# Moving one large store from the Pool queue to the SP queue in a mixture-of-experts kernel

## The chip, the cores and the metric

The kernel runs on one core of one Trainium2 chip. The metric is the device time of one execution in microseconds (us); the kernel before takes 181.32 us, the median of three runs that lie between 181.3 and 181.46. The profile is one further execution taken with the hardware profiler. Its span runs from the first to the last instruction of the core, 179.7 us, a little less than the device time (181.48 us for that execution).

The engines are TensorE (PE, matrix products, with PEld for the loading of its stationary operand), VectorE (DVE), ScalarE (ACT), GpSimd (POOL) and SyncE (SP). Transfers between the chip's main memory and the on-chip memory are issued here by Pool, whose transfers run in a software-made queue (q0 in the profile), or by SP, whose transfers run in a hardware-made queue (q1).

## The reference

Eight experts, each a pair of matrix products with a ReLU between them. Inputs and outputs are fp32.

```python
n_experts, capacity, hidden, expert_hidden = 8, 256, 512, 2048
x:  (8, 256, 512)
w1: (8, 512, 2048)
w2: (8, 2048, 512)

def reference(x, w1, w2):
    h = np.matmul(x, w1)
    h = np.maximum(h, 0)
    return np.matmul(h, w2).astype(np.float32)
```

The weights are 2 x 8 x 512 x 2048 x 4 bytes = 67 MB, which have to be read once; x and the output are 4.2 MB each.

## The kernel before

Pool issues all weight loads. They cast fp32 to bf16 on the way. The experts are loaded in pairs, with the last pair split into single experts and the last w2 into two halves; `tail` is the second half of w2 of expert 7, held back from the list.

```python
GROUPS = [(0, 1), (2, 3), (4, 5), (6, 7)]
W1_LOADS = [(g,) for g in GROUPS[:-1]] + [((6,),), ((7,),)]
W2_LOADS = [(g, 0, K2) for g in GROUPS[:-1]] + [((6,), 0, K2), ((7,), 0, 8), ((7,), 8, K2)]
# ... (cut)
x_v   = x.rearrange("e (pp r) k -> (e pp) (r k)", r=R)
w2_v  = w2.rearrange("e (p j) n -> p e (j n)", p=P)
out_v = out.rearrange("e (p mo) k -> p e (mo k)", mo=MC)
# ... (cut)
out_sb   = const.tile([P, E - 1, MC, H], FP32, name="out_sb")    # experts 0 to 6
out_last = const.tile([P, MC, H], FP32, name="out_last")         # expert 7

def load_w2(es, a, b):
    # ... (cut: picks the group's tile)
    nc.gpsimd.dma_start(
        w2t[g][:, i:i + len(es), a * H:b * H],
        w2_v[:, es[0]:es[-1] + 1, a * H:b * H],
    )

def store_first():
    nc.gpsimd.dma_start(
        out_v[:16, 0:5:2, :16], out_sb[:16, 0:5:2, 0, :16]
    )

def store():
    nc.gpsimd.dma_start(
        out_v[:, :E - 1, :], out_sb[:].rearrange("p e m h -> p e (m h)")
    )
```

`store_first` is the small store: 16 partitions, three experts, 16 numbers each, 3 KB. It writes to a part of the output that `store` writes again, so `store` has to wait until the small store has landed. `store` is the big store: the outputs of experts 0 to 6, 3584 KB, one contiguous row of 4 KB for each partition and expert.

The second layer accumulates over k = 0 to 15 in two row blocks m. For the last expert k is the outer loop, so the tail (k = 8 to 15) is needed from the middle on:

```python
if last:
    order = [(k, m) for k in range(K2) for m in range(MC)]
else:
    order = [(k, m) for m in range(MC) for k in range(K2)]
for k, m in order:
    nc.tensor.matmul(o_ps[m][:], hT[:, k, m * P:(m + 1) * P],
                     w2t[g][:, e - g[0], k * H:(k + 1) * H],
                     start=(k == 0), stop=(k == K2 - 1))
    if k == K2 - 1:
        if last and m == 1:
            nc.scalar.copy(out_last[:, m, :], o_ps[m][:])
        elif last:
            nc.vector.tensor_copy(out_last[:, m, :], o_ps[m][:])
        else:
            nc.vector.tensor_copy(out_sb[:, e, m, :], o_ps[m][:])
```

The main loop, in which the orders of Pool and of TensorE are as written:

```python
nc.sync.dma_start(x_head[:], x_v[:, :HEAD * H])
# ... (cut)
for i, g in enumerate(GROUPS):
    # ... (cut: loads issued as buffers come free; first layer of pairs)
    for e, hT in zip(g, hs):
        layer2(e, hT or layer1(e))
        if e == 5:
            issue(E, E)            # all remaining loads but the tail
            store_first()
            loads.append(tail)
            issue(E, E)            # the tail
        if e == E - 2:
            store()
nc.sync.dma_start(out_v[:, E - 1, :], out_last[:].rearrange("p m h -> p (m h)"))
```

So Pool's queue ends with: loads, small store, tail, big store. SP issues two transfers: a part of x at the start and the last expert's output at the end.

Of the kernel before, what the change touches and what calls it, by code (L numbers as in the profile page):

```python
# [14 lines left out]
def kernel(  # L15
# [7 lines left out]
    nc = tc.nc  # L23
# [69 lines left out]
        )  # L93

    def store():
        nc.gpsimd.dma_start(  # L96
            out_v[:, :E - 1, :], out_sb[:].rearrange("p e m h -> p e (m h)")
        )

# [38 lines left out]
    def layer2(e, hT):  # L138
# [7 lines left out]
        for k, m in order:  # L146
# [7 lines left out]
            if k == K2 - 1:  # L154
# [3 lines left out]
                    nc.vector.tensor_copy(out_last[:, m, :], o_ps[m][:])  # L158
                else:
                    nc.vector.tensor_copy(out_sb[:, e, m, :], o_ps[m][:])  # L160

    loads = []
# [19 lines left out]
    with tc.manual_schedule(engines={mybir.EngineType.PE, mybir.EngineType.Pool}):  # L184
        load_x()
        make_identity(nc, identity)
        issue(B, B - 1)
        transpose_x()
        for i, g in enumerate(GROUPS):
            issue(i + B, i + B)  # L190
            whole = len(g) > 1 and (g,) in W1_LOADS
            if whole:
                hs = [layer1(e) for e in g]
                issue(i + 1 + B, i + B)
            else:
                hs = [None] * len(g)
# [3 lines that stand above are left out]
                    issue(E, E)  # L200
                    store_first()
                    loads.append(tail)
                    issue(E, E)
                if e == E - 2:
                    store()
# [30 lines left out]
```

## Time and profile before

| What | Value |
|---|---|
| device time, median of 3 | 181.32 us |
| span of the profiled execution | 179.7 us |
| TensorE busy | 127.1 us (71%) |
| ScalarE busy | 44.1 us (25%) |
| VectorE busy | 16.5 us (9%) |
| read from main memory | 71.30 MB |
| written to main memory | 4.20 MB |
| share of q0 (Pool) in the 16 transfer engines' span | 96.8% |
| share of q1 (SP) | 2.4% |

The page cuts the span into 40 slices of 4.49 us. A digit is the busy share of a slice in tenths; the rate in GB/s counts bytes as written. A line of the chain of waits gives shares of the span by what the chain passed through. A line of the list of issues gives the tile and tensor, the issuing queue, the count, the size of each and the us from issue to landing. A line of the timeline gives start, duration, engine, source line and operation, and in brackets the idle time before it with what ended it. A line of the transfer records gives the queue, its packets, MB and its share of the 16 engines in the window asked for.

In the kernel before, L91 is the small store, L83 the loads of w2, L96 the big store, L147 the matmuls of the second layer, L160 the copies of experts 0 to 6 into out_sb, L206 the store of the last output.

### The profile page before, as it was taken

The page shows a single profiled execution, that of the slowest core. Times are in us where ns is not written, and L with a number is a line of the kernel's source. Part 1 is how long each engine was busy: PE and PEld are TensorE (multiplying, and loading weights), DVE is VectorE, ACT ScalarE, POOL GpSimd, SP SyncE. Part 2 cuts the span into 40 slices and gives each one's busy share as a digit, 9 for nine tenths or more (in the row PEclk, how much of TensorE's full clock was granted, in tenths as well). Part 3 has the DMA queues.
Part 4 walks back from the last instruction along what each step waited for, and adds up shares of the span by engine and source line. Part 5 has one row for each costly group of instructions (what it writes and reads, how often), then busy time and mean ns, then how long its engine had stood idle before and what let it go on. Part 6 is the DMA issues. An engine that isn't in the chain of part 4 may idle for free.

```text
span 179.7 us, 1827 instructions
## 1 busy us (share of the span) xinstructions
PE 127.1 (71%) x824; PEld 90.5 (50%) x832; DVE 16.5 (9%) x20; ACT 44.1 (25%) x70; POOL 9.9 (6%) x20
## 2 busy tenths in 40 slices
PE   0017600899629991999569943999199999999960
PEld 0017500699514440899434412999034479469520
DVE  0205500000001111000002210000002210110010
ACT  2004400266500000266500000566100026116210
POOL 7000100000100001000100030000002000002000
PEclk9999975699978999699999997899969999999998
DMA  6999998999999899999999999999999999999995
GB/s 201 252 219 204 233 230 186 226 233 208 201 233 230 190 222 233 208 201 233 230 193 219 233 208 201 233 230 193 219 233 204 204 233 228 195 210 214 349 420 217
DMA packets 3735, 40.48 MB, mean 225 GB/s; under 512 B 272, under 2 KB 272, under 8 KB 1296
## 3 DMA queue, kind: packets, MB, share of 16 engines
q0 software_dynamic: 3440, 38.80, 96.8%
q1 hardware_dynamic: 288, 1.57, 2.4%
q8 instruction: 6, 0.10, 0.2%
q14 instruction: 1, 0.01, 0.0%
HBM read 71.30 MB, written 4.20 MB: 420 GB/s over the span
## 4 chain that ended last, share of the span: by engine, by line
PE 58%; DMA 27%; another core or an unknown queue 9%; POOL 1%; issue 1%; ACT 0%; POOLq 0%
PE o_ps L147 32%; DMA w_sb<-in_w_dram 27%; PE h_ps L124 25%; POOL w_sb L76 0%; POOL w_sb L69 0%; ACT out_last L156 0%; POOL identity masks.py:199 0%; POOL identity masks.py:197 0%; POOLq masks.py:199 0%; POOLq L220 0%
## 5 line engine op out<-in xcount | busy, mean ns | idle before, releaser
L124 PE MATMUL h_ps<-xT,w_sb 128*128 128x256 bf16 x512 | 61.3, 285 | 20.2 <-DMA w_sb<-in_w_dram 20.2
L124 PEld LDWEIGHTS <-w_sb 128*128 128x128 bf16 x512 | 58.3, 146 | 24.1 <-DMA w_sb<-in_w_dram 21.9
L147 PE MATMUL o_ps<-w_sb,hT 128*128 128x512 bf16 x248 | 58.6, 393 | 12.8 <-DMA w_sb<-in_w_dram 12.2
L131 ACT ACTIVATE hT<-h_ps 128x512 bf16<-128x512 f32 x64 | 38.2, 597 | 106.8 <-PE h_ps L124 106.8
L147 PEld LDWEIGHTS <-hT 128*128 128x128 bf16 x256 | 25.6, 101 | 44.3 <-issue 9.3
L160 DVE COPY out_sb<-o_ps 128x512 f32<-128x512 f32 x14 | 9.7, 692 | 128.7 <-PE o_ps L147 128.7
L107 PE MATMUL xt_ps<-identity,w_sb 128*128 128x128 bf16 x64 | 7.7, 309 | 13.8 <-DVE w_sb L183 6.9
L107 PEld LDWEIGHTS <-w_sb 128*128 128x128 bf16 x64 | 6.7, 145 | 14.6 <-DVE w_sb L183 6.9
L111 ACT COPY xT<-xt_ps 128x1024 bf16<-128x1024 bf16 x4 | 4.0, 1012 | 16.5 <-PE xt_ps L107 16.5
L83 POOL DMA_DIRECT2D w_sb<-in_w_dram x6 | 3.8, 637 | 53.6 <-PE o_ps L147 36.5
L113 DVE COPY xT<-xt_ps 128x1024 bf16<-128x1024 bf16 x4 | 4.9, 1224 | 10.2 <-PE xt_ps L107 10.2
L76 POOL DMA_DIRECT2D w_sb<-in_w_dram x5 | 3.3, 658 | 44.6 <-PE h_ps L124 44.6
L96 POOL DMA_DIRECT2D out_dram<-out_sb x1 | 1.0, 968 | 27.3 <-issue 27.3
L91 POOL DMA_DIRECT2D out_dram<-out_sb x1 | 0.6, 554 | 29.2 <-DVE out_sb L160 29.2
L156 ACT COPY out_last<-o_ps 128x512 f32<-128x512 f32 x1 | 0.6, 585 | 6.3 <-PE o_ps L147 6.3
L158 DVE COPY out_last<-o_ps 128x512 f32<-128x512 f32 x1 | 0.7, 692 | 13.4 <-PE o_ps L147 13.4
L183 DVE CAST w_sb<-x_head 128x2048 bf16<-128x2048 f32 x1 | 1.2, 1228 | 5.6 <-DMA x_head<-in_x_dram 5.6
L111 ACT ACT_TABLE_LOAD x1 | 1.3, 1283 | 0.7 <-PEq L220 0.7
L69 POOL DMA_DIRECT2D w_sb<-in_x_dram x1 | 0.7, 679 | 0.8 <-POOLq L220 0.8
masks.py:199 POOL TENSOR_SCALAR_AFFINE_SELECT identity<-identity 128x128 bf16<-128x128 bf16 x1 | 0.3, 287 | 0.1
masks.py:197 POOL MEMSET identity<- 128x128 bf16 x1 | 0.2, 223 | 0.0
L220 POOL MEMSET const-float32-0.0<- 128x1 f32 x1 | 0.1, 93 | 0.2 <-issue 0.2
(3 smaller groups left out, 0.3 us busy)
## 6 DMA issues: line engine op xcount, KB each, us to landing
w_sb<-in_w_dram POOLq DMA_DIRECT2D x6, 4096.0 KB, 62.1
w_sb<-in_w_dram POOLq DMA_DIRECT2D x3, 2048.0 KB, 51.5
out_dram<-out_sb POOLq DMA_DIRECT2D x1, 3584.0 KB, 12.9
w_sb<-in_w_dram POOLq DMA_DIRECT2D x2, 1024.0 KB, 44.7
w_sb<-in_x_dram POOLq DMA_DIRECT2D x1, 1536.0 KB, 11.6
x_head<-in_x_dram SPq DMA_DIRECT2D x1, 1024.0 KB, 4.8
out_dram<-out_last SPq DMA_DIRECT2D x1, 512.0 KB, 4.3
out_dram<-out_sb POOLq DMA_DIRECT2D x1, 3.0 KB, 27.8
```

What stands on the lines that cost most here:

```text
L69: nc.gpsimd.dma_start(x_sb[:, HEAD * H:], x_v[:, HEAD * H:])
L76: nc.gpsimd.dma_start(w1t[g][:, i:i + len(es), :], w1_v[:, es[0]:es[-1] + 1, :])
L83: nc.gpsimd.dma_start(w2t[g][:, i:i + len(es), a * H:b * H], w2_v[:, es[0]:es[-1] + 1, a * H:b * H],)
L96: nc.gpsimd.dma_start(out_v[:, :E - 1, :], out_sb[:].rearrange("p e m h -> p e (m h)"))
L107: nc.tensor.transpose(ps[:, r2, :], x_r[:, r2, m, :, ko], identity[:])
L111: nc.scalar.copy(dst, src)
L113: nc.vector.tensor_copy(dst, src)
L124: nc.tensor.matmul(h_ps[:, s, :], w1_r[:, ko, :, j], xT[:, ko, :, e, :], start=(ko == 0), stop=(ko == K1 - 1),)
L131: nc.scalar.activation(hT[:, pr * 2:pr * 2 + 2, :].rearrange("p a c -> p (a c)"), h_ps[:].rearrange("p a c -> p (a c)"), mybir.ActivationF ...
L147: nc.tensor.matmul(o_ps[m][:], hT[:, k, m * P:(m + 1) * P], w2t[g][:, e - g[0], k * H:(k + 1) * H], start=(k == 0), stop=(k == K2 - 1),)
L160: nc.vector.tensor_copy(out_sb[:, e, m, :], o_ps[m][:])
L183: nc.vector.tensor_copy(x_sb[:, :HEAD * H], x_head[:])
```

## The change

The big store is issued by SP instead of Pool. Its place among the calls, its source and its target stay. It still has to wait until the small store has landed, as both write the same rows, and until VectorE has copied expert 6. What it is for: Pool's queue holds the tail between the small store and the big store; from SP's queue the big store can start when the small store has landed, beside the tail. On SP it stands ahead of the store of the last output.

```diff
     def store():
-        nc.gpsimd.dma_start(
+
+
+        nc.sync.dma_start(
             out_v[:, :E - 1, :], out_sb[:].rearrange("p e m h -> p e (m h)")
         )
```

Everything else is the same but for blank lines, which move the line numbers. TensorE, VectorE and ScalarE get the same instructions in the same order; Pool has one transfer less and SP one more.

## The prediction

> **What bounds the kernel now.** I read the slices of the page first, then the chain of waits, the list of transfers by issue, the timeline of the last 45 us, and last the transfer records in short windows around the two points where the queues meet.
>
> ```profile
> PE   0017600899629991999569943999199999999960
> DMA  6999998999999899999999999999999999999995
> GB/s 201 252 219 204 233 230 186 226 233 208 201 233 230 190 222 233 208 201 233 230 193 219 233 208 201 233 230 193 219 233 204 204 233 228 195 210 214 349 420 217
> PE 58%; DMA 27%; another core or an unknown queue 9%; POOL 1%; issue 1%; ACT 0%; POOLq 0%
> ```
>
> The reader is to see that the transfer engines are at 9 tenths in practically every slice and that TensorE has holes. The chain names TensorE for 58%, but that is work hung between arrivals of weights; the transfers never rest. The rate counts bytes as written, and the weights are cast from fp32 to bf16 on the way, so 233 GB/s of weights is 466 GB/s read. In slices 38 and 39 the rate is 349 and 420: there the seven stored outputs pass, fp32 to fp32. A kernel whose transfers are full from the second slice to the last ends when the sum of the bytes has passed, in whatever order, unless the order leaves a hole.
>
> ```profile
> out_dram<-out_sb POOLq DMA_DIRECT2D x1, 3584.0 KB, 12.9
> w_sb<-in_w_dram POOLq DMA_DIRECT2D x1, 1024.0 KB, 32.0
> out_dram<-out_last SPq DMA_DIRECT2D x1, 512.0 KB, 4.3
> out_dram<-out_sb POOLq DMA_DIRECT2D x1, 3.0 KB, 27.8
> ```
>
> These are the issues after 130 us, the last number being us from issue to landing. With the starts on the timeline they give four landings:
>
> ```profile
> 136.36 0.55 POOL L91 DMA_DIRECT2D out_dram<-out_sb  x1 [29.16 <-DVE out_sb L160]
> 136.91 0.57 POOL L83 DMA_DIRECT2D w_sb<-in_w_dram  x1
> 164.73 0.97 POOL L96 DMA_DIRECT2D out_dram<-out_sb  x1 [27.26 <-issue]
> 166.80 7.07 PE L147 MATMUL o_ps<-w_sb,hT 128*128 128x512 bf16 x31
> 174.51 0.35 SPq L206 DMA_DIRECT2D out_dram<-out_last  x1
> ```
>
> The small store lands at 136.36 + 27.8 = 164.2, the tail (second half of w2 of expert 7) at 136.91 + 32.0 = 168.9, the big store at 164.73 + 12.9 = 177.6, the last expert's output at 174.51 + 4.3 = 178.8. The span ends at 179.7. So the big store waits for the small one already: Pool issues it 0.6 us after the small store lands. It then stands behind the tail in the same queue.
>
> **What the Trainium skill says.** "DMA: Bandwidth & Descriptors", section "Issuing engines are not separate DMA queues", says that copies started by the sync and gpsimd engines run on the same 16 transfer engines and interleave, so another issuer saves issue time only. The same page, section "Queues, rings and completion order", says that each transfer engine goes round-robin between its queues, a packet at a time. The trace agrees where the last output meets the big store, in 176 to 177 us:
>
> ```profile
> q1 hardware_dynamic: 68, 0.27, 64.8%
> q0 software_dynamic: 46, 0.16, 38.2%
> ```
>
> Both queues move at once, and the two shares together are full. The page's section "Specifications" gives a first-byte latency of about 0.6 us on the sync path and 1 us on the gpsimd path. The trace is longer: the SP issue at 174.51 shows its first packets in the window 175.6 to 175.8, which is 1.1 us.
>
> **The change part by part.**
>
> Removed: one Pool issue of 0.97 us at 164.73. Pool has nothing after it, so the 0.97 us lie beside everything else. Worth 0.
>
> Added: one SP issue. The order of instructions and their waits in both kernels says that SP now waits for the small store's completion and for the last DVE copy into out_sb, as Pool did. The second comes at 159.63 + 0.69 = 160.3, so the small store at 164.2 ends the wait. SP was idle there (its wait for DVE lasted 173.3 us). SP needs about 0.4 us for such an issue (0.35 for the last output).
>
> Moved: the big store goes from the software queue q0, where each engine reaches it only after its share of the tail, to the hardware queue q1, where it meets the tail. First packets at 164.2 + 1.1 to 1.3 = about 165.4. Before, packets under 8 KB (the store's) first show up in number at 167. So the store begins on a typical engine 2 us earlier, but at the cost of the tail.
>
> How much does the tail lose? It is 128 packets of 8 KB as written, 8 on each engine. In 163.5 to 166.5 the queue ran 89 packets, 9 of them tiny, so 80 in 3 us on 16 engines: 48/80 = 0.60 us each, 4.8 us for 8. The store is 7 x 128 = 896 packets of 4 KB; in 169 to 174 the queue ran 509 of them, 80/509 = 0.157 us each.
>
> ```profile
> DMA packets 509, 2.08 MB, mean 417 GB/s; under 512 B 0, under 2 KB 0, under 8 KB 509
> DMA packets 89, 0.66 MB, mean 219 GB/s; under 512 B 9, under 2 KB 9, under 8 KB 9
> ```
>
> The tiny packets of the small store are spread from 162 to 164 us: the engines stand up to 2 us apart. The last one starts its tail near 164.0 and ends near 164.0 + 4.8 = 168.8, which fits the landing at 168.9. At 165.4 that engine has (168.8 - 165.4)/0.60 = 5.7 tail packets left. If one store packet goes in after each, the tail lands 5.7 x 0.157 = 0.9 us later, at 169.8.
>
> When does TensorE need it? The last expert's second layer starts at 166.80 with 32 matmuls at 7.07/32 = 0.221 us; the tail holds k = 8 to 15, so the first use is matmul 17 at 166.80 + 16 x 0.221 = 170.3. Slack 170.3 - 168.9 = 1.4 us, of which 0.9 is used. TensorE still ends at 173.9 and SP still issues the last output at 174.5.
>
> The end: all but the 512 KB of the last output is in the queues long before it is issued, and after 164 us the engines are full until about 177. The big store and the last output then stand in one queue, the second behind the first, where they interleaved before. Their bytes are the same and so is their sum. The one thing I credit is the changeover from tail to store, where the engines' shares were 0.94 and 0.93 in 167 to 169: 0.06 + 0.07 = 0.13 us of holes, filled when two queues overlap. Sum: 0 - 0.13 + 0 = about -0.1 us, that is 181.2.
>
> **The rivals.**
>
> 1. The tail is delayed past its slack. If the engines share time and not packets, or if a store packet in q1 is several rows long, the last engine needs up to twice its remaining 3.4 us: the tail lands at 172.3, TensorE stalls 172.3 - 170.3 = 2.0 us, and the last output is issued at 176.5. It needs 1.1 us to its first packet, and the rest of its 4.3 us, shared with no one, is at least 512 KB at about 420 GB/s, 1.25 us, plus some 1.2 us to land: 180.1 instead of 178.8. That would make about 182.5. For it speaks that the engines lie so far apart and that the slack is only 1.4 us. Against it speaks 176 to 177 us, where the two queues had 68 and 46 packets of like size, not blocks of one queue.
>
> 2. The hardware queue carries a store of 896 rows more slowly than the software queue. Evidence is thin: alone, q1 has only carried 1 MB at the start and 0.5 MB at the end. At 5% slower the store costs 0.05 x 896 x 0.157/16 = 0.4 us, all of it at the end: 181.7.
>
> 3. Mixing helps more than the holes. Loads write half of what they read, stores do not; if the two kinds overlap inside an engine better than one kind alone, the 3.4 us of overlap could give up to 0.5 us: 180.8. Against it: each engine's share is full with either kind.
>
> 4. Nothing at all, as the store was released by the same event before, and bytes in a full queue are only reordered: 181.3. The main estimate differs from this one by 0.1 us only.
>
> **Range and chances.** Main estimate and rival 4 together 60%, rival 1 in some part 20%, rival 2 10%, rival 3 10%. The predicted time is 181.2 us. The low end takes rival 3 with a little more, 180.5; the high end takes rival 1 nearly whole, 182.3. Two per cent is 3.6 us, more than any of these; faster by over 2% gets 0.02, within 0.95, slower 0.03.
>
> **What would show it right or wrong.** Right: SP's big issue at about 164.2; its first packets near 165.4; the tail landing between 169.3 and 170.3; no wait for weights before matmul 17 of the last expert; TensorE's end at 173.9; the last output landing at 178.6 to 178.9. Rival 1 shows as an idle piece of TensorE inside the last second layer with a tail landing after 170.3. Rival 2 shows as store packets longer than 0.157 us on q1 and as an unchanged start of the last output with a later landing. Rival 3 shows as an earlier landing of the last output with TensorE's end unchanged. What would make all of it wrong is a shift ahead of 164 us, where the two kernels have the same instructions on TensorE, DVE and ACT.

## The result, and the profile after

The changed kernel takes 182.12 us (median of 6 runs, 181.62 to 182.25) beside 181.44 us for the kernel before on the same chip. The ratio is 1.0032, 95% interval 1.0017 to 1.0046: a small loss, some 0.6 us, where I had expected a gain of 0.1. The profiled execution happened to be the quickest of the six (181.62 us), so its profile shows less of the loss than a typical execution does.

From the page of the changed kernel (L149 are the second-layer matmuls, L98 the big store, L207 the last output):

```profile
PE   0017600899939991999479934999199999999960
DMA  5999998999999899999989999999999899999995
GB/s 200 251 219 204 233 233 175 233 233 204 204 233 233 182 226 233 211 197 233 233 189 219 233 215 193 233 233 197 211 233 219 189 233 231 195 213 210 353 422 208
PE 58%; DMA 27%; another core or an unknown queue 9%; POOL 1%; issue 1%; ACT 0%; POOLq 0%
```

The picture is the one of before: full transfer engines and the same chain. The difference has to be looked for in the last 16 us. The issues after 130 us, and the timeline:

```profile
out_dram<-out_sb SPq DMA_DIRECT2D x1, 3584.0 KB, 13.6
w_sb<-in_w_dram POOLq DMA_DIRECT2D x1, 1024.0 KB, 32.6
out_dram<-out_last SPq DMA_DIRECT2D x1, 512.0 KB, 4.7
out_dram<-out_sb POOLq DMA_DIRECT2D x1, 3.0 KB, 27.9
```

```profile
136.16 0.56 POOL L91 DMA_DIRECT2D out_dram<-out_sb  x1 [29.17 <-DVE out_sb L162]
136.70 0.57 POOL L83 DMA_DIRECT2D w_sb<-in_w_dram  x1
...
164.11 0.39 SPq L98 DMA_DIRECT2D out_dram<-out_sb  x1
166.51 7.07 PE L149 MATMUL o_ps<-w_sb,hT 128*128 128x512 bf16 x32
...
174.22 0.34 SPq L207 DMA_DIRECT2D out_dram<-out_last  x1
```

The small store lands at 136.16 + 27.9 = 164.1 and SP issues at once. The tail lands at 136.70 + 32.6 = 169.3. TensorE runs its 32 matmuls in 7.07 us without a stall. The last output is issued 0.3 us earlier than before and lands 4.7 us later instead of 4.3, at 178.9.

The first surprise is in the transfer records. The first line below is the window 164.5 to 167, the other two 167 to 168:

```profile
q0 software_dynamic: 66, 0.54, 103.5%
...
q1 hardware_dynamic: 52, 0.21, 52.6%
q0 software_dynamic: 18, 0.07, 37.8%
```

No row of the store moves before 167, 2.9 us after its issue, although the last output needed only 1.1 us. The first rows begin within 0.01 us of the first completion packets of the tail (167.07 us), so on the engines that are early there is no alternation with the packets of the tail.

### The profile page after: what moved, and what is told of

Same layout as the page of the kernel before. It is cut to its first block, busy times and chain, and to the rows that moved or that the text cites. A ratio compares the mean times of both kernels' runs of the same rounds, so it can differ in the third digit from the quotient of the medians.

```text
span 179.8 us, 1836 instructions
## 1 busy us (share of the span) xinstructions
PE 129.0 (72%) x832; PEld 91.2 (51%) x832; DVE 16.5 (9%) x20; ACT 44.1 (25%) x70; POOL 8.9 (5%) x19
## 4 chain that ended last, share of the span: by engine, by line
PE 58%; DMA 27%; another core or an unknown queue 9%; POOL 1%; issue 1%; ACT 0%; POOLq 0%
PE o_ps L149 33%; DMA w_sb<-in_w_dram 27%; PE h_ps L126 25%; POOL w_sb L76 0%; POOL w_sb L69 0%; ACT out_last L158 0%; POOL identity masks.py:199 0%; POOL identity masks.py:197 0%; POOLq masks.py:199 0%; POOLq L221 0%
## 5 line engine op out<-in xcount | busy, mean ns | idle before, releaser
L126 PE MATMUL h_ps<-xT,w_sb 128*128 128x256 bf16 x512 | 62.8, 289 | 20.3 <-DMA w_sb<-in_w_dram 20.2
L126 PEld LDWEIGHTS <-w_sb 128*128 128x128 bf16 x512 | 59.1, 147 | 24.8 <-DMA w_sb<-in_w_dram 21.9
L149 PE MATMUL o_ps<-w_sb,hT 128*128 128x512 bf16 x256 | 59.2, 393 | 10.5 <-DMA w_sb<-in_w_dram 10.5
L149 PEld LDWEIGHTS <-hT 128*128 128x128 bf16 x256 | 25.6, 101 | 42.5 <-DMA w_sb<-in_w_dram 7.8
L109 PEld LDWEIGHTS <-w_sb 128*128 128x128 bf16 x64 | 6.6, 143 | 14.5 <-DVE w_sb L184 6.8
L91 POOL DMA_DIRECT2D out_dram<-out_sb x1 | 0.6, 557 | 29.2 <-DVE out_sb L162 29.2
## 6 DMA issues: line engine op xcount, KB each, us to landing
out_dram<-out_sb POOLq DMA_DIRECT2D x1, 3.0 KB, 27.9
```

The costliest lines, as they stand in the source:

```text
L109: nc.tensor.transpose(ps[:, r2, :], x_r[:, r2, m, :, ko], identity[:])
L126: nc.tensor.matmul(h_ps[:, s, :], w1_r[:, ko, :, j], xT[:, ko, :, e, :], start=(ko == 0), stop=(ko == K1 - 1),)
L149: nc.tensor.matmul(o_ps[m][:], hT[:, k, m * P:(m + 1) * P], w2t[g][:, e - g[0], k * H:(k + 1) * H], start=(k == 0), stop=(k == K2 - 1),)
```

## The experiments

The kernel before is timed beside each of them; a ratio is to that. The edits are shown shortened.

**The changed kernel once more**, no edit.

> The changed kernel once more, unaltered, for a second profile: the first one was of its fastest execution (181.6 us, while the median is 182.1). Theory A (the store delays the tail): the tail lands 0.5 us or more later after the small store than the 4.7 us of the kernel before, in a typical execution past the first use at matmul 17 of the last expert, and TensorE shows an idle piece there; ratio 1.002 to 1.005. Theory B (the last output waits behind the big store in SP's queue): no idle piece, the issue of the last output as before, but its landing 0.3 to 0.7 us later after the issue than the 4.3 us of before. Theory C (the hardware queue moves the 896 rows more slowly): the rows on q1 take more than 0.159 us each in 169 to 174 us.

Ratio 1.0034 (1.0022 to 1.0045). TensorE has no idle piece in the last second layer. The tail lands 32.9 us after its issue, the last output 4.9 us after its own. Rows on q1 take 159 ns, as rows on q0 did. So theory C (rows slower on SP's queue) falls; of theory A (the store delays the tail until TensorE waits) the late tail is there and the wait is not. And a new thing shows. The window 165 to 166.8 holds only tail packets. Packets x mean = share x 16 engines x 1.8 us, so the mean can be read off. First the kernel before, then this run, then the first profile of the change:

```profile
q0 software_dynamic: 48, 0.39, 104.2%
```

```profile
q0 software_dynamic: 46, 0.38, 107.8%
```

```profile
q0 software_dynamic: 48, 0.39, 104.2%
```

That is 30.0/48 = 625 ns before and 31.0/46 = 675 ns here. The last packets of the tail have become slower, before any row of the store is recorded. The first profile, of the quickest execution, reads as the kernel before does: there only five tail packets are long, and they start at 166.95 to 167.24, outside the window. The slowing differs from one execution to the next.

**The last output from ScalarE's queue.**

```diff
-    nc.sync.dma_start(out_v[:, E - 1, :], out_last...)
+    nc.scalar.dma_start(out_v[:, E - 1, :], out_last...)
```

> The changed kernel with the last output issued by ScalarE, so that it has a queue of its own and alternates with the big store again. Theory B: the loss goes, ratio to before 0.999 to 1.001. Theories A and C: no gain from it, ratio 1.002 to 1.005 as for the changed kernel.

Ratio 1.0026 (1.0015 to 1.0038). Theory B (the last output waits behind the big store in SP's queue) falls: a queue of its own doesn't take the loss away.

**The big store in two pieces.**

```diff
-        nc.sync.dma_start(out_v[:, :E - 1, :], ...)
+        for a, b in ((0, 1), (1, E - 1)):
+            nc.sync.dma_start(out_v[:, a:b, :], out_sb[:, a:b]...)
```

> The big store cut into expert 0 (128 rows) and experts 1 to 6 (768 rows), both on SP behind the small store. In the changed kernel the first row moved 2.9 us after the issue, against 1.1 us for the 128 rows of the last output. If the number of rows sets this start-up time, expert 0's rows start 1.1 to 1.4 us after the issue, at about 165.4, between the tail's packets, the tail lands up to 0.9 us later than in the kernel before, and by theory A the ratio is 1.003 to 1.008. If the queue of the loads holds the store back until the tail has been taken in, nothing of expert 0 moves before 167 and the ratio is that of the changed kernel.

Ratio 1.0019 (1.0009 to 1.0029). The 128 rows of expert 0, issued at 163.92, don't move before 166.9 either. The number of rows is not what delays them. That the loss is somewhat smaller than the changed kernel's 1.0034 is not explained.

**The small store behind the tail.**

```diff
                     issue(E, E)
-                    store_first()
                     loads.append(tail)
                     issue(E, E)
+                    store_first()
```

> The changed kernel with the small store issued after the tail, so that the big store on SP starts only when the tail has landed, at about 168.9. Theory A: the tail keeps its 4.7 us and TensorE its end, but the transfer engines stand empty from about 167.5 to 170 or 172 (1.1 to 2.9 us after the issue), so the end comes 1.5 to 3 us later, ratio 1.008 to 1.017. Theory C: rows on q1 are slow even with no load beside them. If the loss is neither of these but a hole after the small store, the ratio is near 1.

Ratio 1.0106 (1.0091 to 1.0122), a hole as expected. The use of this run is the start-up time with nothing in the way: issued at 169.70, its 896 rows begin at 170.6, after 0.9 us. The other 2 us of the changed kernel pass while packets of the loads run. That an engine has taken these packets in before it looks at the other queue would fit, but no run shows what an engine holds.

**Half of the store behind the tail in Pool's queue.**

```diff
                     loads.append(tail)
                     issue(E, E)
+                    nc.gpsimd.dma_start(out_v[:, 1:6:2, :], ...)
...
-        nc.sync.dma_start(out_v[:, :E - 1, :], ...)
+        nc.sync.dma_start(out_v[:, 0:7:2, :], ...)
```

> Experts 1, 3 and 5 are stored by Pool, at once behind the tail in its queue; only experts 0, 2, 4 and 6 go to SP behind the small store. On each engine the tail is then followed by store rows of its own queue, as in the kernel before, and rows of SP's queue follow rows of Pool's. Theory D (time is lost on an engine when rows of SP's queue pass beside the last packet of the loads; only the six engines that run about 1 us late lose it): no loss, ratio 0.999 to 1.001, all tail packets at 625 ns, tail landing 32.0 us after its issue. Theory C' (a row issued by SP costs more somewhere, whatever it follows): 4/7 of the loss stays, ratio 1.0015 to 1.0025. If SP's rows come in between the tail's packets all the same, the tail is late as in the changed kernel and the loss stays whole.

Ratio 1.0033 (1.0023 to 1.0043), the tail lands after 32.8 us instead of 32.0, and its packets in 165 to 166.8 average 28.8 x 1.058/43 = 709 ns:

```profile
q0 software_dynamic: 43, 0.35, 105.8%
```

Theories D and C' both miss: the loss is whole although the tail is followed by rows of its own queue. Those rows had been issued at 146.84, and still no tail packet is long before 165.2, 1 us after SP's issue of the other half at 164.25.

**No small store, big store on SP.** The edit takes the call `store_first()` out.

> The changed kernel without the small store, which leaves out nothing of the result: the big store on SP is released by the copy of expert 6 at about 160.3, its rows could move from about 161.3, when each engine has one packet of the first half of w2 and all 8 of the tail left. If queues alternate packet by packet, rows appear at 161 to 162 on all engines, the tail lands 9 x 0.159 = 1.4 us or more later, TensorE stalls by up to some tenths of a us, and by theory D the loss grows, ratio 1.004 to 1.012. If an engine first empties what it has taken in from the loads' queue, rows appear at about 163 or only at 167, and the ratio is that of the changed kernel, 1.002 to 1.004.

Ratio 1.0017 (1.0009 to 1.0025). SP issues at 158.60; the loads' packets are longer from 159.7 to 162.5, and the first rows come at 162.3, 3.7 us after the issue. From then on rows and tail packets alternate, and a tail packet takes 624 ns again. So the slowed packets here are not the last ones of the tail: all but at most one lie in the load before it. The tail is so late that TensorE waits:

```profile
170.93 3.61 PE L149 MATMUL o_ps<-w_sb,hT 128*128 128x512 bf16 x16 [1.25 <-DMA w_sb<-in_w_dram]
```

The stall of 1.25 us, which as my first rival I had charged to the end of the kernel, costs little: by then most of the store has gone, and the last output lands 3.8 us after its issue.

**No small store, big store on Pool: the control.** The same edit in the kernel before.

> The kernel before without the small store: Pool issues the big store at about 160.5 instead of 164.7, still behind the tail in the same queue. Control for the run on SP without the small store: the store waits its turn behind the tail, which ends at 168.9 as before. Ratio 0.998 to 1.001 by every theory.

Ratio 1.0035 (1.0022 to 1.0047). This miss decided the matter. SP has no part in the end of this run but for the last output, the store stands behind the tail in one queue, and the loss is as large as that of the change. The window 165 to 166.8:

```profile
q0 software_dynamic: 41, 0.34, 108.4%
```

31.2/41 = 761 ns for a tail packet. What this run shares with the changed kernel is only that the store is ready early, here since 160.71 + 0.96 = 161.7:

```profile
160.71 0.96 POOL L96 DMA_DIRECT2D out_dram<-out_sb  x1 [50.32 <-DVE out_sb L160]
```

The slowed packets begin at 165.2, not before. In the kernel before Pool is through with its issue at 164.73 + 0.97 = 165.7, 1.2 us before the first rows move.

**Four experts stored at 106 us.**

```diff
-                    store_first()
...
-                if e == E - 2:
-                    store()
+                if e == E - 2:
+                    store(4, 7)
+                if e == 3:
+                    store(0, 4)
```

> No small store; SP stores experts 0 to 3 as soon as expert 3 is done, at about 109 us, with some 50 us of loads waiting in Pool's queue, and experts 4 to 6 after expert 6. Shows how an engine shares two queues when the loads' queue can't run empty. If they alternate packet by packet, the 32 rows of each engine pass within 32 x (0.62 to 1.25 + 0.159) = 25 to 45 us of the issue; if the loads' queue goes first, they pass only when it runs empty, after 160. The last loads land 4/7 of 8.9 us = 5.1 us later, TensorE ends 5.1 - 1.4 = 3.7 us later, and only 3/7 of the store is left beside it: ratio 1.010 to 1.022 if rows alternate, 1.002 to 1.006 if they wait. By theory D many rows beside loads cost extra, so the upper part of the range.

Ratio 1.0236 (1.0222 to 1.025), somewhat above the range: TensorE also waits for w1 of the last expert. Its worth is the picture of two queues that both have work. The window 120 to 140:

```profile
q0 software_dynamic: 251, 3.85, 90.1%
q1 hardware_dynamic: 245, 1.00, 13.1%
```

One row of 4 KB for each load packet of 16 KB: the engines share by packets and not by time. No load packet is slowed in this stretch. Nor is the wait before it like that of the other runs: the rows, issued at 106.14, first move at 110.0, and of the 32 load packets that start in 107 to 110 the longest takes 1.32 us against 1.23. A store that stands ready doesn't slow every load ahead of it; here the load packets are of 16 KB and 512 rows stand ready, and which of these matters wasn't tried.

**The release of the store moved.** Theory F: what counts is how long the store stands ready while an engine works on its last packets of the tail. In these four kernels there is no small store; ScalarE copies 16 columns of expert 6's last block after ReLU number n (counted from 0) of the eight of expert 7, and the store waits for that. For this ScalarE's order is fixed by hand as well.

```diff
+            if e == E - 1 and pr == n:
+                nc.scalar.copy(out_sb[:, e - 1, 1, H - 16:], held[0][:, H - 16:])
+                store()
...
+                elif (e, m) == (E - 2, 1):
+                    nc.vector.tensor_copy(out_sb[:, e, m, :H - 16], o_ps[m][:, :H - 16])
+                    held.append(o_ps[m])
```

On Pool (n = 3, the fourth ReLU):

> The store stays on Pool, behind the tail and with no small store, as in the run that measured 1.0035 with the issue at 160.7; only its release moves: 16 columns of expert 6's last block are copied by ScalarE after the fourth of the eight ReLUs of expert 7, at about 164.2, so that Pool issues at about 164.4 (164.7 in the kernel before). Theory F (the last packets of the tail are slowed while the store's rows already stand in a queue; in the kernel before the rows come just in time): nearly no tail packet over 640 ns, ratio 0.999 to 1.0015. Theory G (the small store itself, cutting the loads apart, is what the kernel before gains by): ratio 1.0025 to 1.0045 again.

On SP, n = 4:

> The big store on SP without the small store, released by ScalarE after the fifth ReLU of expert 7, so that SP issues at about 165.3, 1.2 us later than in the changed kernel; its rows could move from 166.2, the first engines finish the tail at about 166.9. Theory F: fewer slowed tail packets than the changed kernel, ratio 1.000 to 1.002. Theories C' and G: 1.0025 to 1.004.

On SP, n = 5:

> The same with the release after the sixth ReLU: SP issues at about 166.1, rows could move from 167.0, just as the first engines finish the tail. Theory F: hardly any slowed tail packet, ratio 0.999 to 1.001, equal to the kernel before; the ten early engines may lose 0.1 us in waiting for rows. Theories C' and G: 1.0025 to 1.004.

On SP, n = 7:

> The release goes after the last ReLU of expert 7: SP issues at about 167.0, rows could move from 167.9 to 168.0, some 0.9 us after the ten early engines have finished the tail and about when the six late ones do. If only the late engines set the end, the early ones' empty 0.9 us cost nothing: ratio 0.999 to 1.002, no slowed tail packet. If every engine's empty time counts, 10/16 x 0.9 = 0.6 us is lost: ratio 1.003 to 1.005.

Pool: 1.0005 (0.9997 to 1.0014). SP, n = 4: 1.0003 (0.9995 to 1.0012). SP, n = 5: 0.9999 (0.9989 to 1.0009). With n = 5 SP issues at 165.31; its line of the timeline, and the window 165 to 166.8:

```profile
165.31 0.39 SPq L99 DMA_DIRECT2D out_dram<-out_sb  x1
...
q0 software_dynamic: 47, 0.39, 102.0%
```

29.4/47 = 625 ns, the undisturbed packet. Same transfer, same queue as in the changed kernel, 1.1 us later: the loss is gone. On Pool a shift of 3.0 us takes 1.0035 to 1.0005; the issue with n = 3 and the same window:

```profile
163.71 0.96 POOL L97 DMA_DIRECT2D out_dram<-out_sb  x1 [54.60 <-ACT out_sb L138]
...
q0 software_dynamic: 47, 0.39, 104.7%
```

30.2/47 = 642 ns. Theory G (the small store itself) and C' (SP's queue) are out: without the small store, and on SP, the kernel is as quick as before. One rival is untested. No run copies the 16 columns on ScalarE and still releases the store early, so it isn't excluded that this edit does some of the good; that the slowed packets go from 9 (Pool, ready, that is through with the issue, at 164.7) over 3 (SP, ready at 165.3) to none (SP, ready at 165.7) speaks for the release.

With n = 7 the rows come too late, 1.0027 (1.0014 to 1.0039), which lies between my two expectations and doesn't separate them: the issue fell at 167.38 and the rows began at 168.3, when nearly all engines had run dry, the late ones too. The rows are dearer as well (below).

The runs side by side, without the two that let the store in after the tail or at 106 us. The packet columns are counted in the transfer records of one profile each: tail packets (for the run without the small store on SP also those of the load before it) longer than 640 ns, and the time above 625 ns of such packets, divided by 16. The next column is explained below the table. The time is that of the profiled execution itself, the ratio that of all executions.

| Run | issue of the store, us | first row, us | slowed packets | excess per engine, us | loss of the six late engines, us | time of this execution, us | ratio |
|---|---|---|---|---|---|---|---|
| before | Pool 164.73 | 166.9 | 0 | 0 | 0 | 181.48 | 1 |
| SP, n = 5 | SP 165.31 | 167.1 | 0 | 0 | -0.04 | 181.41 | 0.9999 |
| SP, n = 4 | SP 164.85 | 166.9 | 3 | 0.01 | 0.01 | 181.26 | 1.0003 |
| Pool, n = 3 | Pool 163.71 | 167.0 | 9 | 0.07 | 0.14 | 181.62 | 1.0005 |
| changed, first profile | SP 164.11 | 167.1 | 5 | 0.06 | 0.18 | 181.62 | 1.0032 |
| changed, again | SP 164.20 | 167.1 | 11 | 0.14 | 0.27 | 181.90 | 1.0034 |
| last output on ScalarE | SP 164.23 | 167.0 | 14 | 0.15 | 0.44 | 182.07 | 1.0026 |
| two pieces | SP 163.92 | 166.9 | 17 | 0.13 | 0.28 | 181.50 | 1.0019 |
| no small store, SP | SP 158.60 | 162.3 | 35 | 0.22 | 0.19 | 181.64 | 1.0017 |
| half on Pool | Pool 146.84, SP 164.25 | 167.2 | 27 | 0.32 | 0.51 | 182.14 | 1.0033 |
| no small store, Pool | Pool 160.71 | 167.2 | 32 | 0.42 | 0.52 | 182.04 | 1.0035 |
| SP, n = 7 | SP 167.38 | 168.3 | 0 | 0 | 0.46 | 181.90 | 1.0027 |

**Why a small excess reaches the end.** The transfer engines are not abreast. Each load ends with one small completion packet on each of the 16 engines. In the kernel before, around the end of a load, the window 127.5 to 129 and then 129 to 130.5:

```profile
DMA packets 28, 0.26 MB, mean 175 GB/s; under 512 B 12, under 2 KB 12, under 8 KB 12
...
DMA packets 20, 0.26 MB, mean 175 GB/s; under 512 B 4, under 2 KB 4, under 8 KB 4
```

Twelve engines are on time and four are about a microsecond late. At 11 to 13 us all 16 are together, and at 50 us one is late. The page's third part has six packets of a queue named instruction, 16 KB each; here is one of them, in the window 37 to 38.5:

```profile
q0 software_dynamic: 15, 0.25, 76.7%
q8 instruction: 1, 0.02, 3.7%
```

It holds an engine for 0.037 x 16 x 1.5 = 0.89 us. The records carry no engine numbers, but the counts go together: after one of these packets one engine is late, after four there are four, and at the end six engines complete the last output after 177.6 us:

```profile
DMA packets 28, 0.09 MB, mean 64 GB/s; under 512 B 6, under 2 KB 6, under 8 KB 28
```

So the early ten end about 1 us before the span's transfers do, and the late six set the end. In the table their loss is the mean time from the completion of w1 of expert 7 to the last completion, against the kernel before. In the second profile of the change it is 0.27 us and the longest such time grows by 0.3, while the ten early engines lose nothing in the mean. That is most of the 0.4 us by which that profile's span, 180.1, exceeds 179.7. Across the table, the two pieces excepted, the loss of the late engines goes with the time of the same execution: it is 0 within 0.04 us in executions of 181.26 to 181.48 us, 0.14 to 0.19 in those of about 181.63, and 0.27 to 0.52 in those of 181.90 to 182.14.

## Why the prediction was right or wrong

The measured 182.12 us lay in the range, but the sign of the main estimate was wrong. That the range held it is luck: its high end, 182.3, stood for rival 1, a stall of TensorE, and the time came near it without a stall.

- *Release by the small store at 164.2, SP idle and quick*: right, issue at 164.11.
- *Removal of Pool's issue worth 0*: right as to its 0.97 us. Wrong in what I did not weigh: this issue, with Pool's 0.6 us of delay before it, kept the rows out of the queue until 165.7.
- *First rows about 165.4, one after each tail packet, tail at 169.8*: wrong. Rows moved from 167.1. The tail was late (169.3, and 32.9 us after its issue in the second profile) through longer packets in the main; rows that came in between number about five in the second profile (21 rows of 172 ns, 16 of which are the first on their engine), too few to matter. (An undisturbed tail packet takes 625 ns, not the 0.60 us of the working.) I had read 68 and 46 packets in 176 to 177 as two queues alternating on an engine. In part they belong to different engines: ten were through with the store (its completion packets come at 175.6 to 176.3), six were not (176.8 to 177.3). With the last output in ScalarE's queue the same picture comes again.
- *TensorE unhindered, last output issued as before*: right, and rival 1 (a stall) with its cost wrong: where a stall did come it cost a fraction of itself.
- *Same rows, same cost in either queue* (against rival 2): right, 159 ns.
- *Changeover holes of 0.13 us filled, total -0.1 us*: this is the step that failed. The 0.13 us were the wrong term: instead of filling holes, the store that stands ready early goes with slower packets at the end of the tail, 675 ns on average instead of 625 in the second profile, and the end moves by +0.6 us. Rival 4, mere reordering, fails for the same reason; rival 3 has the wrong sign.

What stays open: why a waiting store slows the packets ahead of it. The runs show that it happens with either queue, that a later release takes it away with either queue, and that it ends once rows alternate. They don't show why, nor why 16 KB load packets were hardly slowed at 107 to 110. Nor is timing the whole of it: Pool with n = 3 is ready at 164.7 and the changed kernel at 164.6, and their ratios are 1.0005 and 1.0034. With one or two profiles of each kernel, the sizes aren't explained either: the excess grows from 0.14 to 0.42 us where the ratio hardly moves.

## What to carry to other kernels

In this kernel, whose transfers are full to the end, issuing the store earlier had no gain to fetch, and it cost: let the store become ready shortly before the engines run out of loads. Here SP's issue 1.8 and 2.1 us before the first rows cost nothing (n = 5, n = 4), 3 us before cost 0.3% (the change), and an issue about when the early engines ran out cost about as much (n = 7). Compare an issuer with the same issue time on the other queue before crediting the issuer. None of the versions beat the kernel before; the best, SP with n = 5, equals it.

## What was not expected of the hardware

- The store issued by SP began 0.9 us after the issue on idle engines (store behind the tail) and 1.8 to 3.9 us after it where loads were running (n = 5: 165.31 to 167.1; four experts at 106: 106.14 to 110.0). Where both queues had work for long, packets alternated one for one, 4 KB rows against 16 KB packets (245 against 251; 229 of these rows took 172 ns, as the first rows behind a load packet do in the change, and not the 159 ns of rows that follow one another). "DMA: Bandwidth & Descriptors", section "Queues, rings and completion order", speaks of turns of some 9 to 17 descriptors; here a turn was a single row.
- One of the 16 KB packets of the queue named instruction took 0.89 us, and as many engines then ran about 1 us late as such packets had passed, until the others had to wait for them (with n = 7 all 16 complete the store within 0.4 us). "Runtime: NRT & Kernel Launch", section "Instruction fetch mechanics", calls the cost of crossing such a 16 KiB block mostly hidden; here the six late engines end the kernel. That the packets are this refill is read from their queue's name and size.
- Where all engines started the store at almost the same moment, with n = 7, a row took 5 x 16 x 1.019/500 = 163 ns in 170 to 175 us, against 5 x 16 x 1.028/517 = 159 ns with n = 5, where they started up to 1.4 us apart.
